# Other estimates of instruction time, by which a planned kernel orders its side work

## Chip, cores and metric

The kernel runs on one core of one Trainium2 chip. The metric is device time in microseconds (us) of one execution. The core has five engines with a queue each: TensorE (PE, matrix products into PSUM), VectorE (DVE), ScalarE (ACT), GpSimd (POOL) and SyncE (SP), which starts transfers.

## What is computed

One layer of a hybrid backbone for 1024 latent tokens and 256 context tokens of width 1024, in single precision. Cut to what matters:

```python
h_l = rmsnorm(x_l) * (1 + mod[1]) + mod[0]         # latents; h_c likewise for the context
parts = split(h @ w_in)                            # one combined input projection
lru = lru_branch(...)    # 8 blocks of 128 channels, both directions, first-order recurrence
gdn = gdn_branch(...)    # gated DeltaNet, 8 heads, chunks of 64, both directions
ssd = ssd_branch(...)    # Mamba-2 scan, 16 heads in 2 groups, chunks of 128, both directions
x_l = x_l + mod[2] * (sum(sigmoid(gate[k]) * (branch[k] @ w_branch[k]) for k in range(3)) @ w_out)
x_l = x_l + mod[5] * hier_moe(rmsnorm(x_l))        # top 2 of 32 experts, 1024 -> 512 -> 1024
out = rmsnorm(x_l)
```

In the gated DeltaNet each chunk solves a triangular system and then passes a 128x128 state on to the next chunk, so that the chunks of a head form a chain.

## The kernel before

A projection with single precision is made of three matmuls for each of 8 row tiles (high and low parts, names `hhi`, `hlo`, `whi`, `wlo`; PSUM tile `pj`, for the context `chi`, `clo` and `pjc`). A block is 128 columns of the weight: 48 matmuls of 512 columns for the latents, 24 of 256 for the context. These blocks are the main work of PE in the first part of the program (`phase1`): LRU blocks, context part of GDN, SSD group 0, SSD group 1, GDN heads, gates, merge. At most two latent PSUM tiles are held at a time.

All else there is side work, written as Python generators that yield between steps: convolutions (`conv`), LRU gates and scans (`lru_scan`: gate matmuls `psg`), inverses of the chunks' triangles (`gdn_inverse`: small matmuls `p`, `po`, `pz`), the chunk chains of a GDN head (`gdn_chain`, `gdn_steps`: matmuls `ch`, DVE steps `z`, `S`, `o`, ScalarE steps `w`), SSD tiles (`ssd_intra`: masks `gm` on GpSimd, matmuls `parg`, `py`, products `L`).

Which step stands where in the program is decided when the program is built, by `Clock`. Every engine call goes through a helper (L256, so that nearly all rows of the profile name this line), which first books an estimated time: an instruction starts when its engine, its inputs and its output buffer are free, and takes `cost`; its result is ready 0.1 us later. After every three projection matmuls of a row tile `mmblock` calls `tick`, which issues the next step of each side task whose last step, by the estimates, is done by PE's time:

```python
            g, r, m = e
            if r + m > clk.now:
                continue
```

Here `m` is `MARGIN` = -0.1 us and a new task begins with `r` = 0.0. Where PE's own work can't go on (both PSUM tiles held in `run`, a flag awaited in `until`, a stage's end in `drain`), `tick(True)` moves PE's estimated time on to the next side step. Everything issued to an engine's queue then runs in that order on the chip, whatever the real times are. The second part (routing, experts, combination) is ordered without these estimates.

Of the kernel before, what the change touches and what calls it, by code (L numbers as in the profile page):

```python
# [12 lines left out]
F32R = mybir.dt.float32r  # L13
# [5 lines left out]
PSUM = bass.MemoryType.PSUM  # L19
DRAM = bass.MemoryType.DRAM  # L20

P = 128
# [8 lines left out]
FX = 3  # L31
DB = 4
# [112 lines left out]
class Clock:  # L145
    """Estimated times (us) at which the engines and the tiles are free of the instructions issued so far; the order
    in which independent pieces of work are issued goes by them."""

    TABLES = (("Tanh", "Exp"), ("Gelu_apprx_tanh", "Tanh"), ("Silu", "Tanh"), ("Sqrt",), ("Sigmoid", "Tanh"))

# [13 lines left out]
    def cost(self, eng, op, out, kw, ins):  # L164
        n = out.free_size()
        if eng == "tensor":
            if op == "transpose":
                return 0.12
            c = kw["rhs"].free_size()
            return c / 2400 if kw["rhs"].dtype == F32R else max(4 * c / 2400, 0.06)  # L170
        if eng == "vector":
            if op == "reciprocal":
                return 0.07 + n * 6.3e-3
            if op == "tensor_reduce":
                n = ins[0].free_size()
            psum = any(a.space == PSUM for a in ins)
            fast = op in ("tensor_copy", "tensor_scalar") and not psum
            return (0.13 if psum else 0.07) + n * (0.53e-3 if fast else 1.05e-3)
        if eng == "scalar":
            f = str(kw.get("func")).split(".")[-1]  # L180
            c = 0.13 + 0.75e-3 * n
            if any(f in t for t in self.TABLES) and f not in self.table:
                self.table = next(t for t in self.TABLES if f in t)
                c += 1.28
            return c
        if op == "indirect_dma_start":
            return 1.0
        return 0.1 + n * {"tensor_tensor": 2.2e-3, "affine_select": 1.05e-3}.get(op, 3.5e-3)

    def issue(self, eng, op, args, kw):  # L190
# [13 lines left out]
        else:  # L204
            t += self.cost(eng, op, outs[0], kw, ins)
            self.t[eng] = t
            t += 0.1
# [10 lines left out]
class TimedPool:  # L218
    """a tile pool; keeps book of when the buffers that its tiles take over are free."""
# [50 lines left out]
class Core:  # L270
# [15 lines left out]
    # ---------------------------------------------------------------- consts  # L286
# [24 lines left out]
    def softplus(self, out, x, pool, shape, name):  # L311
        """max(x, 0) + log(1 + exp(-|x|)), the logarithm as 2 atanh(e / (2 + e))."""
# [20 lines left out]
    # ------------------------------------------------------------ projection  # L333
    def mmblock(self, ps, hi, lo, rhs, n, mid=None, kouter=False, gate=None):
        """ps[:, :n] = W^T @ rhs, W = hi + lo, rhs(k) = (hi, lo) of row tile k."""
# [16 lines left out]
    def run(self, jobs):  # L352
        """jobs: callables, or (weight block, kind, done); done(block, psum tile, is latent)."""
# [19 lines left out]
    def give(self, ps):  # L373
        """a projection's PSUM tile is not needed any more."""
        big = ps.free_size() == SEQ
        self.live[big] -= 1
        if not big:
            self.aux.free(ps)

    def bank(self, name):  # L380
        """a bank of PSUM that is kept across steps, until it is given back."""
# [4 lines left out]
    def room(self):  # L386
        """until a bank of PSUM is free."""
# [5 lines left out]
    def tick(self, idle=False):  # L393
        """next steps of the side tasks whose last steps are done by now; idle: the tensor engine has nothing else."""
# [26 lines left out]
    def take(self, pool, tag, n=1):  # L421
        """wait until n buffers of the tag are free, and count them as used until they are given back."""
# [13 lines left out]
    # ---------------------------------------------------------------- adaLN  # L436
    def mod_rows(self):
        """adaLN parts 2..5 of the latent stream, as rows in DRAM."""
# [44 lines left out]
    def start(self, xp):  # L483
        """adaLN scale and shift, norm, and the hi / lo parts of both transposed streams."""
# [121 lines left out]
    def gate_jobs(self, n):  # L606
        """jobs of the next n merge gate blocks."""
# [4 lines left out]
    # ------------------------------------------------------------------ LRU  # L612
# [14 lines left out]
    def lru_conv(self, b, ps, wts):  # L627
        """one block of 128 channels; columns: context, then latents."""
# [23 lines left out]
    def lru_scan(self, b, d, u, wts, hs):  # L652
        """gates and recurrence of one direction."""
# [80 lines left out]
    # ------------------------------------------------ decays, steps and betas  # L734
# [18 lines left out]
    def smalls(self, ps, n, t0, lat):  # L753
        """gate inputs of GDN and SSD for token tiles t0.. (tokens on partitions)."""
# [69 lines left out]
    def small_done(self):  # L824
        """the space of the gate inputs' temporaries goes to the merge gates."""
# [9 lines left out]
    # ------------------------------------------------------------------ SSD  # L835
# [9 lines left out]
    def ssd_block(self, b, ps, n, lat, dst, flag):  # L845
        """conv + silu of one xbc block, into a channel-major tile and / or token-major columns."""
# [34 lines left out]
    def ssd_update(self, pool, g, d, T, xs, bt, st):  # L881
        """state of direction d after token tile T (global tile index)."""
# [15 lines left out]
    def ssd_ctx_jobs(self, g):  # L898
        """context states of one group."""
# [35 lines left out]
    def ssd_intra(self, g, T, s, t0):  # L935
        """the part of a token tile's output that comes from the tile itself, both directions at once."""
# [46 lines left out]
        # 128 columns wide: the second half is overwritten by the head that it belongs to  # L983
# [6 lines left out]
    def ssd_scan(self, g, d, t0):  # L990
        """state chain of one direction and the output that comes from it."""
# [94 lines left out]
    def ssd_jobs(self, g, n):  # L1086
        """one group of 8 heads; n gate blocks run beside its scan."""
# [29 lines left out]
    # ------------------------------------------------------------------ GDN  # L1117
    def gdn_pool(self, tc, lat):
        """the context has room for two inverses at a time."""
# [9 lines left out]
    def gdn_fixed(self):  # L1129
        """lhsT tiles of the triangular inverses: zero outside the blocks that are written."""  # L1130
# [13 lines left out]
    def gdn_block(self, cb, ps, n, out, flag):  # L1144
        """conv + silu of one block into out [P, n]."""
# [8 lines left out]
    def gdn_keys(self, bt, norms=True, keys=True):  # L1154
        """token-major keys, their norms."""
# [36 lines left out]
    def gdn_decays(self, bt):  # L1192
        """decays between the tokens of a tile, both directions at once; the factors of keys by keys and queries."""
# [58 lines left out]
    def gdn_pre(self, bts, vflags, done):  # L1252
        """what two batches of 4 token tiles need that does not depend on the state; the inverses run beside."""
# [13 lines left out]
    def gdn_inverse(self, bt):  # L1267
        """Y = (I + B)^-1: 16-blocks by substitution, then block merges 16 -> 32 -> 64 -> 128."""
# [85 lines left out]
        # 32 -> 64; the forward direction fills the odd quadrants, the backward one the even ones  # L1354
# [29 lines left out]
        # 64 -> 128  # L1384
# [23 lines left out]
    def gdn_steps(self, sts):  # L1408
        """one token tile of every scan of sts, in step: the products first, then all that reads them."""
# [52 lines left out]
    def gdn_ctx_proj(self):  # L1462
        """context keys and values of all heads, kept in DRAM."""
# [11 lines left out]
    def gdn_ctx_jobs(self):  # L1475
        """context states of all heads."""
# [36 lines left out]
    def gdn_chain(self, h, bts, og):  # L1513
        """the scans of a head; og: outputs of the tiles 0, 1, 6 and 7, and of the tiles between, which are done first."""
# [31 lines left out]
    def gdn_out(self, h, bts, og, zs):  # L1546
        """norm and output gate of a head."""
# [35 lines left out]
    def gdn_jobs(self, n):  # L1583
        """n[0] gate blocks beside the preparation of the first head, n[1 + h] beside the scan of head h."""
# [57 lines left out]
    # ---------------------------------------------------------------- merge  # L1642
# [134 lines left out]
    # ------------------------------------------------------------------ MoE  # L1777
# [31 lines left out]
    def route_tokens(self, a, b):  # L1809
        """groups, experts and weights of the token tiles a to b - 1."""  # L1810
# [48 lines left out]
    def route(self, rp):  # L1859
        """slots of the assignments.  # L1860
# [656 lines left out]
```

## Time and profile before

| what | before |
| --- | --- |
| median of 3 runs | 3391.51 us (3386.56 to 3393.18) |
| profiled execution, span from its first to its last instruction | 3387.1 us |
| the same execution against the runs' median | 4.4 us below it |
| PE busy | 2976.2 us, 88% |
| DVE busy | 2251.0 us, 66% |
| ACT busy | 1553.5 us, 46% |
| POOL busy | 772.1 us, 23% |
| mean granted TensorE clock | 0.935 of full speed |

The page gives no time for the profiled execution other than its span, so the span stands for it. Busy shares are averages over stages which differ much; the rows further down are cut by stretch. A matmul's recorded duration includes the time in which the next already runs, so the rate of PE is read from the starts of two neighbours.

### The profile page before, as it was taken

The page shows a single profiled execution, that of the slowest core. Times are in us where ns is not written, and L with a number is a line of the kernel's source. Part 1 is how long each engine was busy: PE and PEld are TensorE (multiplying, and loading weights), DVE is VectorE, ACT ScalarE, POOL GpSimd, SP SyncE. Part 2 cuts the span into 40 slices and gives each one's busy share as a digit, 9 for nine tenths or more (in the row PEclk, how much of TensorE's full clock was granted, in tenths as well). Part 3 has the DMA queues.
Part 4 walks back from the last instruction along what each step waited for, and adds up shares of the span by engine and source line. Part 5 has one row for each costly group of instructions (what it writes and reads, how often), then busy time and mean ns, then how long its engine had stood idle before and what let it go on. Part 6 is the DMA issues. An engine that isn't in the chain of part 4 may idle for free. (4 is left out here: it accounts for less than half of the span.)

```text
span 3387.1 us, 48583 instructions
## 1 busy us (share of the span) xinstructions
PE 2976.2 (88%) x18570; PEld 2345.0 (69%) x18570; DVE 2251.0 (66%) x5049; ACT 1553.5 (46%) x2188; POOL 772.1 (23%) x662
## 2 busy tenths in 40 slices
PE   7878789879799789879989999899988799999992
PEld 3657667667568557668777778677766588878882
DVE  4676765753744745887988885244544887787786
ACT  4556565424315324454444444311121576676674
POOL 1121221202612611112111111212110243333333
PEclk8989999979799799989999999999989799999996
DMA  4112222201002001001010111454443697887896
GB/s 187 63 56 78 74 76 78 78 24 50 13 32 75 7 26 62 28 21 35 22 34 27 34 47 65 153 195 174 150 145 136 260 361 290 310 337 287 321 354 235
DMA packets 105531, 423.12 MB, mean 125 GB/s; under 512 B 17224, under 2 KB 26568, under 8 KB 79696
## 3 DMA queue, kind: packets, MB, share of 16 engines
q1 hardware_dynamic: 79872, 372.17, 30.5%
q10 hardware_dynamic: 13968, 26.83, 2.1%
q0 software_dynamic: 11456, 21.00, 1.7%
q8 instruction: 147, 2.41, 0.3%
q14 instruction: 88, 0.72, 0.1%
HBM read 381.11 MB, written 59.79 MB: 130 GB/s over the span
## 5 line engine op out<-in xcount | busy, mean ns | idle before, releaser
L256 PE MATMUL pj<-hhi,whi 128*128 128x512 f32 x1488 | 643.8, 433 | 17.8 <-DVE kq L256 10.3
L256 PE MATMUL pj<-hhi,wlo 128*128 128x512 f32 x1488 | 597.7, 402 | 6.9 <-POOL wlo L256 3.7
L256 PE MATMUL pj<-hlo,whi 128*128 128x512 f32 x1488 | 597.4, 401 | 0.0
L256 DVE TENSOR_TENSOR wl<-raw,wh 128x2048 fp32r<-128x2048 f32 x188 | 447.9, 2403 | 103.4 <-ACT wh L256 101.1
L256 POOL TENSOR_TENSOR wlo<-raw,whi 128x1024 fp32r<-128x1024 f32 x78 | 197.1, 2527 | 1002.8 <-ACT whi L256 985.5
L256 ACT ACTIVATE wh<-raw 128x2048 fp32r<-128x2048 f32 x188 | 360.6, 1919 | 129.2 <-PE psu L256 103.2
L256 PEld LDWEIGHTS pj<-hhi,whi 128*128 128x128 f32 x1488 | 286.7, 193 | 77.8 <-issue 10.1
L256 PEld LDWEIGHTS pj<-hhi,wlo 128*128 128x128 f32 x1488 | 285.3, 192 | 78.4 <-POOL wlo L256 5.3
L256 PEld LDWEIGHTS pj<-hlo,whi 128*128 128x128 f32 x1488 | 287.6, 193 | 53.8 <-issue 3.2
L256 ACT ACTIVATE whi<-raw 128x1024 fp32r<-128x1024 f32 x145 | 152.8, 1056 | 293.6 <-PE pj L256 212.8
L256 PE MATMUL psu<-wl,xh 128*128 128x512 f32 x576 | 226.6, 393 | 2.9 <-DVE wl L256 2.9
L256 PE MATMUL psu<-wh,xh 128*128 128x512 f32 x576 | 229.1, 398 | 0.0
L256 PE MATMUL psu<-wh,xl 128*128 128x512 f32 x576 | 226.0, 392 | 1.1 <-DVE xl L256 1.1
L256 ACT ACT_TABLE_LOAD x147 | 188.6, 1283 | 77.0 <-DVE xt L256 32.2
L256 DVE TENSOR_TENSOR wlo<-raw,whi 128x1024 fp32r<-128x1024 f32 x67 | 87.8, 1310 | 185.0 <-ACT whi L256 185.0
L256 ACT ACTIVATE w<-ch,D 128x128 f32<-128x128 f32 x288 | 84.7, 366 | 161.6 <-PE ch L256 155.7
L256 POOL TENSOR_TENSOR yo<-yo,m 128x1024 f32<-128x1024 f32 x35 | 103.6, 2961 | 183.5 <-ACT yo L256 183.4
L256 PE MATMUL psg<-u,lw 128*128 128x512 f32 (+1 forms) x192 | 89.8, 605 | 55.5 <-issue 52.7
L256 PE MATMUL pj<-bh,whi 128*128 128x512 f32 x384 | 122.9, 402 | 12.0 <-DVE acc L256 6.5
L256 PE MATMUL pj<-bl,whi 128*128 128x512 f32 x384 | 122.2, 400 | 8.9 <-POOL bl L256 6.3
L256 PEld LDWEIGHTS psu<-wl,xh 128*128 128x128 f32 x576 | 109.0, 189 | 29.3 <-DVE wl L256 8.0
L256 PEld LDWEIGHTS psu<-wh,xl 128*128 128x128 f32 x576 | 108.8, 189 | 24.7 <-DVE xl L256 1.8
(455 smaller groups left out, 6295.5 us busy)
## 6 DMA issues: line engine op xcount, KB each, us to landing
raw<-in_w SPq DMA_DIRECT2D x188, 1024.0 KB, 6.8
raw<-in_w_in SPq DMA_DIRECT2D x119, 512.0 KB, 3.5
wr<-in_w_mod SPq DMA_DIRECT2D x32, 512.0 KB, 6.0
gate<-gt ACTq DMA_DIRECT2D x48, 256.0 KB, 2.0
raw<-in_w_branch SPq DMA_DIRECT2D x24, 512.0 KB, 3.6
st<-br SPq DMA_DIRECT2D x24, 512.0 KB, 5.5
gt<-gate SPq DMA_DIRECT2D x24, 512.0 KB, 4.5
wm<-in_w_mod SPq DMA_DIRECT2D x8, 1024.0 KB, 5.7
```

What stands on the lines that cost most here:

```text
L256: return f(*args, **kw)
```

## The change

`Clock.cost` gets other formulas, and the time after which a result counts as ready becomes one of each engine. Nothing else in the program's logic changes; the lists of jobs, `MARGIN` and the pools stay. All instructions but one are the same in kind and number (the program has 148 table loads on ScalarE where it had 147); they stand in another order.

```diff
+    LAG = {"tensor": 0.21, "vector": 0.11, "scalar": 0.12, "gpsimd": 0.1, "sync": 0.1}
...
             if op == "transpose":
-                return 0.12
+                return 0.11
             c = kw["rhs"].free_size()
-            return c / 2400 if kw["rhs"].dtype == F32R else max(4 * c / 2400, 0.06)
+            if kw["rhs"].dtype == F32R:
+                return c / 2400 + 0.014
+            rows = kw["lhsT"].partition_size()
+            if "tile_position" in kw:
+                return 0.024 if rows == 32 else 0.055
+            return max(c / 600, 0.11)
+        psum = any(a.space == PSUM for a in ins)
...
+            if op == "tensor_tensor_scan":
+                return 0.08 + n * 2.08e-3
...
-            psum = any(a.space == PSUM for a in ins)
-            fast = op in ("tensor_copy", "tensor_scalar") and not psum
-            return (0.13 if psum else 0.07) + n * (0.53e-3 if fast else 1.05e-3)
...
+            if op in ("tensor_copy", "tensor_scalar", "memset"):
+                c = 0.14 if len(ins) > 1 else 0.09
+                return c + n * (1.04e-3 if psum else 0.52e-3)
+            c = 0.15 if op == "scalar_tensor_tensor" and len(ins) > 2 else 0.09
+            return c + n * 1.04e-3
...
-            c = 0.13 + 0.75e-3 * n
+            c = (0.08 if psum else 0.12) + 0.09 * max(0, len(ins) - 1) + 0.83e-3 * n
+            if kw.get("accum_out") is not None:
+                c += 0.2
...
-                c += 1.28
+                c += 1.38
...
-        return 0.1 + n * {"tensor_tensor": 2.2e-3, "affine_select": 1.05e-3}.get(op, 3.5e-3)
+        if op == "affine_select":
+            return 0.12 + n * 0.9e-3
+        return 0.15 + n * (2.25e-3 if op == "tensor_tensor" else 3.5e-3)
...
-            t += 0.1
+            t += self.LAG[eng]
```

What this moves is seen on PE at three places; the rows are in program order, `pj` and `pjc` are projection matmuls, and the others are side work.

The first place is the fifth LRU head's first gate matmul `psg`. Before, it stands in the middle of a block, after 999 projection matmuls, and the second gate follows one row tile later:

```order
L256 MATMUL pj<-hhi,wlo 128x512
L256 MATMUL psg<-u,lw 128x512 x2
L256 MATMUL psg<-u,lw 128x256
L256 MATMUL pj<-hhi,whi 128x512
L256 MATMUL pj<-hlo,whi 128x512
L256 MATMUL pj<-hhi,wlo 128x512
L256 MATMUL ptr<-ident,xt 128x128 x4
L256 MATMUL psg<-u,lw 128x512 x2
L256 MATMUL psg<-u,lw 128x256
```

In the changed order both stand behind 1032 projection matmuls, at the end of a latent block, and context matmuls follow:

```order
L276 MATMUL pj<-hhi,wlo 128x512
L276 MATMUL psg<-u,lw 128x512 x2
L276 MATMUL psg<-u,lw 128x256
L276 MATMUL ptr<-ident,xt 128x128 x2
L276 MATMUL psg<-u,lw 128x512 x2
L276 MATMUL psg<-u,lw 128x256
L276 MATMUL pjc<-chi,whi 128x256
L276 MATMUL pjc<-clo,whi 128x256
```

So 33 projection matmuls moved ahead of `psg`, and the two gates of the head stand together behind them.

The second place is the end of SSD group 0's projections. Before, the first two tiles' products `py` stand between the last row tiles:

```order
L256 MATMUL parg<-gm,mr 128x512 x4
L256 MATMUL pj<-hhi,whi 128x512
L256 MATMUL pj<-hlo,whi 128x512
L256 MATMUL pj<-hhi,wlo 128x512
L256 MATMUL py<-xs,L 128x128 x7
L256 MATMUL py<-xs,L 128x64
L256 MATMUL pj<-hhi,whi 128x512
L256 MATMUL pj<-hlo,whi 128x512
L256 MATMUL pj<-hhi,wlo 128x512
L256 MATMUL py<-xs,L 128x128 x7
L256 MATMUL py<-xs,L 128x64
```

In the changed order `py` stands behind the last projection matmul of the group, with the next tiles' `pcb` and `pcs` behind it:

```order
L276 MATMUL parg<-gm,mr 128x512 x4
L276 MATMUL pj<-hhi,whi 128x512
L276 MATMUL pj<-hlo,whi 128x512
L276 MATMUL pj<-hhi,wlo 128x512
L276 MATMUL parg<-gm,mr 128x512 x4
L276 MATMUL py<-xs,L 128x128 x7
L276 MATMUL py<-xs,L 128x64
L276 MATMUL py<-xs,L 128x128 x7
L276 MATMUL py<-xs,L 128x64
L276 MATMUL pcb<-cT,bT 128x128
L276 MATMUL pcs<-sst_178,cT 128x512
L276 MATMUL pcb<-cT,bT 128x128
```

So `py` of the first tiles moved behind the last 12 projection matmuls.

The third place is in the GDN stage, around a block's end after 4200 projection matmuls; `ch` belongs to the chain of one head, `p`, `pq` and `pk` to the next head's preparation. Before, single steps of the chain stand between row tiles ahead of it:

```order
L256 MATMUL ch<-z,Yf_8914 128x128
L256 MATMUL pj<-hhi,whi 128x512
L256 MATMUL pj<-hlo,whi 128x512
L256 MATMUL pj<-hhi,wlo 128x512
L256 MATMUL ch<-w_13635,kt 128x128
L256 MATMUL ch<-w,am 128x128
L256 MATMUL pq<-ident,kq 128x128 x4
L256 MATMUL p_13655<-Z_8917,B 64x64 x8
L256 MATMUL pj<-hhi,whi 128x512
L256 MATMUL pj<-hlo,whi 128x512
L256 MATMUL pj<-hhi,wlo 128x512
L256 MATMUL pk<-ident,kq 128x128 x4
```

In the changed order several steps of the chain stand behind one another at the block's end:

```order
L276 MATMUL pj<-hhi,wlo 128x512
L276 MATMUL ch<-w_13491,kt 128x128
L276 MATMUL ch<-w,am 128x128
L276 MATMUL pot<-ident,o 128x128 x4
L276 MATMUL ch<-S,kq 128x128 x2
L276 MATMUL pq<-ident,kq 128x128 x4
L276 MATMUL ch<-S,kq 128x128 x2
L276 MATMUL p_13591<-Z_13542,B 32x32 x16
L276 MATMUL ch<-z,Yf_8913 128x128
L276 MATMUL pk<-ident,kq 128x128 x4
L276 MATMUL ch<-w_13611,kt 128x128
L276 MATMUL ch<-w,am 128x128
```

So the chain's steps moved from places between projection matmuls to the block's end, where no projection matmul lies between them.

## Rows read from the trace of the kernel before

**Rows 1.** The page: busy time by engine, and the granted clock in 40 slices.
```profile
PE 2976.2 (88%) x18570; PEld 2345.0 (69%) x18570; DVE 2251.0 (66%) x5049; ACT 1553.5 (46%) x2188; POOL 772.1 (23%) x662
PEclk8989999979799799989999999999989799999996
```

**Rows 2.** Busy time by stretch: start:end length, busy us (instructions) by engine, PEclk, DMA.
```profile
40.00:537.00 497.00, 413.65 (x2011) 320.36 (x2011) 337.94 (x432) 285.95 (x374) 96.33 (x44) 0.91 0.21 67
690.00:756.00 66.00, 41.20 (x660) 35.11 (x660) 34.84 (x181) 16.57 (x52) 0.00 (x0) 0.69 0.07 21
867.00:955.00 88.00, 63.22 (x196) 37.41 (x196) 71.87 (x122) 19.64 (x53) 49.64 (x58) 0.78 0.04 12
1330.00:2040.00 710.00, 637.95 (x6902) 518.99 (x6901) 613.02 (x2668) 328.37 (x643) 119.68 (x208) 0.96 0.10 31
1430.00:1530.00 100.00, 79.64 (x1083) 64.92 (x1072) 89.78 (x421) 50.66 (x103) 14.84 (x31) 0.90 0.08 24
1530.00:1630.00 100.00, 99.29 (x840) 82.25 (x832) 78.42 (x297) 43.60 (x87) 21.11 (x34) 1.00 0.11 34
1272.00:2128.00 856.00, 782.30 (x7890) 639.95 (x7889) 681.52 (x2867) 390.73 (x754) 145.16 (x244) 0.97 0.11 36
```

**Rows 3.** Waits of PE, whole run: us in total, times, longest us.
```profile
PE psg L256 <- issue: 52.7, 7, 13.8
```

**Rows 4.** Timeline around psg: start, us, engine, operation [idle before <-releaser].
```profile
357.09 1.52 DVE L256 SCALAR_TENSOR_TENSOR u<-pjc,pp,u 128x254 f32<-128x254 f32 x3 [1.00 <-ACT u L256]
...
358.71 3.75 PE L256 MATMUL psg<-u,lw 128*128 128x512 f32 x4 [13.80 <-issue]
```

**Rows 5.** Waits of PE, then one of DVE, 1272 to 2128 us.
```profile
PE ch L256 <- DVE o L256: 25.1, 26, 3.7
PE pj L256 <- DVE kq L256: 10.3, 3, 6.8
PE pz L256 <- DVE B L256: 4.9, 1, 4.9
PE pz L256 <- DVE at L256: 4.4, 2, 2.5
...
PE ch L256 <- ACT w L256: 2.0, 4, 0.6
...
DVE z L256 <- PE ch L256: 22.8, 21, 10.2
```

**Rows 6.** Waits of PE, 610 to 691 us.
```profile
PE p L256 <- DVE Bc L256: 3.6, 1, 3.6
PE p L256 <- DVE Z L256: 3.4, 5, 1.0
PE p L256 <- DVE Zq L256: 3.1, 1, 3.1
```

**Rows 7.** Timeline of the SSD drain's rounds, POOL and PE.
```profile
853.55 1.27 POOL L256 TENSOR_TENSOR L<-L,t 128x512 f32<-128x512 f32 x1 [2.89 <-ACT L L256]
...
854.87 1.38 PE L256 MATMUL py<-xs,L 128*128 128x128 f32 x10 [0.55 <-POOL L L256]
...
877.54 6.14 PE L256 MATMUL py<-xs,L 128*128 128x128 f32 x32 [2.88 <-POOL L L256]
```

**Rows 8.** Groups by form, 40 to 2517 us; then PE's timeline.
```profile
L256 DVE TENSOR_TENSOR_SCAN ea<-ea,gate 128x1280 f32<-128x1280 f32 x8 | 22.5, 2810 | 0.0
...
L256 DVE SCALAR_TENSOR_TENSOR z<-ch,ge,vp 128x128 f32<-128x128 f32 x144 | 48.6, 344 | 27.3 <-PE ch L256 26.9
...
L256 ACT ACTIVATE w<-ch,D 128x128 f32<-128x128 f32 x288 | 84.7, 366 | 161.6 <-PE ch L256 155.7 <-DMA sgd<-Sc 5.5
...
L256 POOL TENSOR_SCALAR_AFFINE_SELECT gm<-shi 128x512 fp32r<-128x512 f32 x64 | 46.5, 726 | 5.0 <-PE parg L256 5.0
...
341.25 0.40 PE L256 MATMUL pj<-hhi,whi 128*128 128x512 f32 x1
...
341.72 0.39 PE L256 MATMUL pj<-hhi,wlo 128*128 128x512 f32 x1
```

More of the change, by code (lines that the diff above doesn't have):

```diff
@@ L173, in cost @@
                 return 0.07 + n * 6.3e-3
+            if op == "tensor_tensor_scan":
+                return 0.08 + n * 2.08e-3
             if op == "tensor_reduce":
-                n = ins[0].free_size()
-            psum = any(a.space == PSUM for a in ins)
-            fast = op in ("tensor_copy", "tensor_scalar") and not psum
-            return (0.13 if psum else 0.07) + n * (0.53e-3 if fast else 1.05e-3)
+                return 0.08 + ins[0].free_size() * 1.04e-3
+            if op == "stream_shuffle":
+                return 0.13 + n * 1.0e-3
+            if op in ("tensor_copy", "tensor_scalar", "memset"):
[3 more added lines that the diff above has]
+            return c + n * 1.04e-3
         if eng == "scalar":
             f = str(kw.get("func")).split(".")[-1]
-            c = 0.13 + 0.75e-3 * n
+            c = (0.08 if psum else 0.12) + 0.09 * max(0, len(ins) - 1) + 0.83e-3 * n
+            if kw.get("accum_out") is not None:
+                c += 0.2
             if any(f in t for t in self.TABLES) and f not in self.table:
                 self.table = next(t for t in self.TABLES if f in t)
-                c += 1.28
+                c += 1.38
             return c
```

## Prediction

> **What bounds the kernel now.** I read the page first, then busy time by stretch, the waits of TensorE (PE), the waits of VectorE (DVE), and last the timeline around the longest waits. On the page PE is busy 2976.2 of 3387.1 us and DVE 2251.0 [rows 1], so PE looks like the bound; but that is an average. By stretch the picture differs [rows 2]. From 40 to 537 us (projections with the LRU beside them) PE is busy 413.65 of 497 us and DVE 337.94. In the drain from 690 to 756 us no projection is left and a chain of small matmuls and DVE steps runs alone: PE 41.20 of 66 us, granted clock 0.69. The same holds for the SSD drain, 867 to 955 us, clock 0.78 (1118 to 1205 us is its copy for the second group). In the GDN stage, 1330 to 2040 us, both engines are close to full: PE 637.95 and DVE 613.02 of 710 us. What the changed numbers can win is the waiting of PE at side instructions that stand too early in its queue, since the projection matmuls behind them wait too; what they can lose is that a side chain starts or ends later where it alone sets the end of a stage. The routing, the experts and the combination (2600 us to the end) don't issue by the estimates, and I take them as unchanged.
>
> **The change, part by part.** The new lines are slower almost throughout, and they slow the side engines more than PE. A projection matmul of 512 columns starts 0.235 us after the one before [rows 8]; the old formula gives 512/2400 = 0.213, the new one 0.227. A DVE scan of 1280 takes 2.810 us; old 0.07 + 1280 x 0.00105 = 1.41, new 0.08 + 1280 x 0.00208 = 2.74. The DVE step z takes 0.344; old 0.26, new 0.28. The ScalarE step w takes 0.366; old 0.23, new 0.28. One line goes the other way: a GpSimd mask of 512 takes 0.726 on average; old 0.64, new 0.58. A result of PE now counts as ready 0.21 us after its end instead of 0.1. So in the estimates DVE work lengthens by more than projections do, and a side step is put behind more projection matmuls than before. No instruction is added but one table load on ScalarE (147 to 148 in the built programs); ScalarE is busy 1553.5 of 3387.1 us [rows 1], so I charge nothing for it, and if nothing covered it, it would cost one load, about a microsecond, below what counts here.
>
> **LRU.** Seven times the first gate matmul psg of a head waits, 52.7 us in all, longest 13.8 [rows 3]. The timeline shows why: at 358.71 us psg starts after an idle time of 13.80 us, just behind the end of the context convolution on DVE, which starts its last part at 357.09 [rows 4]. The new table would put psg behind that wait if it were allowed to. But a new side task enters the list with an estimated end of 0.0, and its first gate comes out right after the convolution's last step was issued; the estimates only decide what DVE work was put ahead of the convolution. I priced the DVE work that stands ahead of it in the new order with durations of the trace: about 3.5, 3.3, 5, 9.8, 8, 1, 9.5 and 12.5 us of waiting for the eight heads, 52.6 in all. I take **-1 us**; bounds -12 (the fourth and fifth lose a good half of their wait) and +8 (the order of the two scans of a head turns against it once).
>
> **Context part of GDN.** Between 610 and 691 us PE waits 3.6, 3.4 and 3.1 us at p matmuls [rows 6], 10.1 in all. In the new order the first group of these stands 48 projection matmuls later (48 x 0.235 = 11.3 us), so these waits go. But the stretch behind is the uncovered drain, and now 348 instead of 328 small matmuls stand in it. The drain's 66 us for 328 matmuls make 0.2 us for each, so 20 more cost 4 us; a batch that starts 11.3 us later may end the stage up to 4 us later still, of which I take all. I take -10.1 + 8 = **-2 us**; bounds -10.1 (the drain's own chain decides) and +6 (the late batch decides: the 16 us of both together, less the 10).
>
> **SSD.** The first two matmul groups py of the drain's chain start at 854.87 us, while projections still run; the next round starts at 877.54 [rows 7], so a round takes some 23 us and the drain is a chain of them: GpSimd's product L ends (853.55 + 1.27), py starts. The first parg stands 12 to 15 projection matmuls later in the new order and py behind the last projection, not 12 ahead of it. PE loses nothing by that, but the chain starts 12 x 0.235 = 2.8 us later, and the rounds behind it are as long as before. I take +2.5 for each of two groups, **+5 us**; bounds 0 (the wait of 0.55 us ahead of py and the projections moved forward hide it) and +8.
>
> **GDN heads.** PE's waits that the order makes are those on o (25.1 us), kq (10.3), B (4.9), at (4.4) and w (2.0) [rows 5], 46.7 us. DVE in turn waits 22.8 us for ch. If every one of these steps stood where its input is ready, 46.7 us would be won; that is the lower bound. Against it, the chain of a head (80 steps ch) spans 1226 projection matmuls in the new order over heads 1 to 7 where it spanned 1064, 162 more or 162 x 0.235 = 38 us, and side matmuls behind the last projection matmul of a block, where nothing covers them, rise from 467 to 891. If this length is paid in full, and only half of the waits other than kq (which is late by itself) come back, the sum is 38 - 18 = +20: the upper bound. The two ends are far apart. DVE is busy 86% of the stage, which leaves neither end whole: 97 us of idle are there to be won from, but the stage can't run much ahead of DVE. I take the middle, -13.
>
> **Merge.** The side work there is DMA-fed modulation rows, priced as before: 0.
>
> **Sum.** -1 - 2 + 5 - 13 = -11 us. Against the profiled execution that is 3387.1 - 11 = 3376.1 of span; the median of the runs, 3391.51, lies 4.4 above that span, so **3380 us**.
>
> **The rivals.** (a) The waits only move. Where a block's last projection is done and its PSUM isn't free, PE waits anyway; 891 side matmuls at block ends could be just the old waits, seen at another place. DVE at 613.02 of 710 us speaks for it, the 46.7 us of PE waits with projections behind them against it. Then GDN gives about 0, and the sum is +2: 3393, no change that can be told.
> (b) Slower: longer chains set the stage ends. The point where it decides is the GDN chain: if a head's chain is paid at its new length, 38 us, and the waits in front of ch come back to half, +20, then with the others the sum is -1 + 6 + 5 + 20 = +30: 3421; with the GDN term at half of that, 3411. For it speaks that steps at the ends of blocks run uncovered, as the drains do; against it that the next head's projections usually wait for the same DVE.
> (c) The clock. Stretches in which PE pauses run slower: from 1430 to 1530 us PE is busy 79.64 us at clock 0.90, from 1530 to 1630 us 99.29 us at 1.00 [rows 2]. If the whole GDN stage fell to 0.90 from its mean of 0.96, PE would lose 0.06 x 710 = 43 us of matmul time, of which its 72 us of idle time absorb a part; I price half, +20, and with no gain left in GDN that is 3393 + 20 = 3413. The Trainium skill, "TensorE: Matmul & The Clock Gate", section "What's actually happening", says that an idle array is gated down from 2.4 to 1.2 GHz; the rows of the two stretches agree, since a granted share of 0.90 is a mix of the two levels. By that rule the 424 more side matmuls at block ends are a danger, and the forecast would come out on the slower side.
> (d) The gain is whole: with GDN near its lower bound, -40, the sum is -38 and the time 3353.
>
> **Chances.** My forecast, 3361 to 3385, 0.36; (d) and beyond, 0.10; (a), 3385 to 3398, 0.25; (b) 0.20; (c) 0.09. A change of under 0.2% (6.8 us) is about what a measurement of this kernel can't tell from none, so the bound between faster and same lies at 3384.7 and that to slower at 3398.3. Faster 0.46, same 0.25, slower 0.29. The likeliest case's own range is 3361 to 3385; the range that holds 8 in 10 leaves out most of (d)'s and the upper part of (b)'s ends: 3350 to 3412.
>
> **What would show it.** In the changed kernel's profile: waits of PE on o in the GDN stage at half of 25.1 us or less, with the stage shorter than 856 us from 1272 to 2128; psg's waits still some 50 us; the waits at p between 610 and 691 us gone and the drain behind them 4 to 8 us longer; first py of the SSD drain behind the last projection, with rounds of 23 us as before. I would be wrong if the ends of blocks in the GDN stage show PE idle for as long as the waits did (a), if the GDN stage is longer than 860 us with its waits gone (b), or if its granted clock falls under 0.94 (c).

## The result, and the profile after

The changed kernel takes 3429.72 us (3427.16 to 3431.9) where the one before takes 3391.74: 1.0117 times as long, 95% interval 1.0105 to 1.0129. That is 38 us slower, on the other side of the forecast and beyond its range. The profiled execution has a span of 3426.6 us.

The page of the changed kernel has nearly the same sums as [rows 1], PE busy 2988.3 us instead of 2976.2 and DVE 2255.8 instead of 2251.0:

```profile
PE 2988.3 (87%) x18570; PEld 2370.3 (69%) x18570; DVE 2255.8 (66%) x5049; ACT 1556.9 (45%) x2189; POOL 769.6 (22%) x662
...
PEclk9989999959799799989899989999989799999996
```

PE has the same 18570 matmuls and is busy 12 us longer with them, as much as its growth in the GDN heads alone (further down); the other 27 us of the 39 by which the span grew are idle time of PE. Where the loss lies is read by the starts of the same projection matmul in both traces (5304 of them, in the same order in both). The table is worked out from the two timelines; "drain" is the time from a stage's last projection matmul to the first of the next stage.

| up to projection matmul | before, us | changed, us | difference | stage's own share |
| --- | --- | --- | --- | --- |
| 1008 (fifth LRU block) | 368.1 | 344.6 | -23.4 | |
| 1656 (LRU done) | 536.7 | 536.7 | 0.0 | 0.0 |
| 2136 (context part of GDN done) | 756.2 | 757.9 | +1.6 | +1.6 (drain 65.5, then 83.4) |
| 3096 (SSD done) | 1204.9 | 1210.2 | +5.4 | +3.8 (first drain 88.6, then 101.1) |
| 3480 (GDN heads begin) | 1321.3 | 1326.5 | +5.2 | -0.2 |
| 5112 (GDN heads nearly done) | 2109.1 | 2139.3 | +30.2 | +25.0 |
| 5303 (last) | 2161.8 | 2192.1 | +30.3 | +0.1 |
| end | 3387.1 | 3426.6 | +39.4 | +9.1 |

Two rows need care. At 1008 the changed kernel hasn't yet had the fifth head's psg wait: before, it stands at 999 (13.8 us), now at 1032 (7.3 us). From 1044 on the changed kernel is 10.9 us ahead, at 1620 it is 4.4, and then the last head's psg waits 13.8 us instead of 6.1. Of the last row's 9.1 us most is scatter, as a run of the old order shows further down.

The same stretches in busy time, as in [rows 2]: LRU, the longer drain of the context part, the first SSD drain, and the heads from 3480 to 5112:

```profile
40.00:537.00 497.00, 410.39 (x2005) 320.41 (x2006) 338.84 (x433) 284.70 (x373) 96.49 (x44) 0.91 0.21 68
674.43:757.86 83.43, 52.32 (x690) 45.16 (x689) 47.88 (x264) 18.58 (x58) 1.27 (x2) 0.59 0.05 17
856.79:957.88 101.09, 73.15 (x254) 43.62 (x253) 83.41 (x141) 25.26 (x69) 58.63 (x69) 0.80 0.04 11
1326.50:2139.30 812.80, 726.09 (x7546) 605.68 (x7544) 656.75 (x2801) 362.69 (x710) 132.33 (x229) 0.93 0.10 32
```

and for comparison the heads before, cut at the same two matmuls:

```profile
1321.30:2109.10 787.80, 714.10 (x7550) 583.28 (x7548) 651.94 (x2803) 361.35 (x712) 132.61 (x229) 0.96 0.10 34
```

The reader is to see that DVE has almost the same work in the heads, 656.75 and 651.94 us, and that its idle time grew from 135.9 to 156.1 us. PE is busy 726.09 us instead of 714.10 and its granted clock fell from 0.96 to 0.93. The heads hold two thirds of the loss.

PE's waits in the heads (PE, what it waits for: us in total, times, longest) answer to [rows 5]:

```profile
PE ch L276 <- DVE o L276: 16.8, 13, 2.7
PE pj L276 <- DVE kq L276: 16.7, 4, 7.9
PE ch L276 <- ACT w L276: 9.8, 13, 1.9
...
PE pz L276 <- DVE at L276: 6.3, 3, 3.7
```

The wait for o fell from 25.1 to 16.8 us, by a third where the prediction looked for half; kq rose from 10.3 to 16.7, w from 2.0 to 9.8 and at from 4.4 to 6.3. The wait for B at pz is gone. So the five waits that the prediction added up, 46.7 us before, are 49.6 now. On the other side DVE waits longer for the chain's matmuls. In the changed kernel, 3480 to 5112:

```profile
DVE z L276 <- PE ch L276: 28.7, 27, 8.2
DVE S L276 <- PE ch L276: 27.0, 27, 2.9
```

and before, the same stretch:

```profile
DVE z L256 <- PE ch L256: 21.2, 18, 10.2
...
DVE S L256 <- PE ch L256: 12.8, 16, 1.7
```

55.7 us now, 34.0 before: 21.7 us more, as much as DVE's idle time grew in all, with the other waits rising and falling among themselves. That these waits are the cause doesn't follow; the experiments with the chain come back to them.

Where PE's time went is seen best at one block's end. After projection matmul 3816 the changed kernel's PE timeline (start, duration, operation) reads

```profile
1467.64 0.40 PE L276 MATMUL pj<-hhi,wlo 128*128 128x512 f32 x1
1467.87 0.38 PE L276 MATMUL ch<-w,kt 128*128 128x128 f32 x2
...
1531.53 0.65 PE L276 MATMUL p<-Z,B 32*32 32x32 f32 x32
1533.30 1.11 PE L276 MATMUL pv<-ident,vT 128*128 128x128 f32 x4 [1.12 <-ACT P L276]
1534.21 1.06 PE L276 MATMUL ch<-S,kq 128*128 128x128 f32 x4
1534.92 0.77 PE L276 MATMUL pj<-hhi,whi 128*128 128x512 f32 x1
```

and before

```profile
1489.68 0.39 PE L256 MATMUL pj<-hhi,wlo 128*128 128x512 f32 x1
...
1516.90 0.71 PE L256 MATMUL pj<-hhi,whi 128*128 128x512 f32 x1
```

The next block's first projection matmul starts 67.3 us after this block's last one, and before 27.2 us. Behind the last one stands side work alone: chain steps and, as the last of it, the next head's p and pv. In that stretch PE is busy 46.22 of 68.90 us at clock 0.76, and DVE 61.85:

```profile
1466.00:1534.90 68.90, 46.22 (x694) 39.13 (x694) 61.85 (x311) 28.47 (x67) 8.77 (x20) 0.76 0.03 9
```

Summed over the 34 block ends between 3480 and 5112, the time above 0.235 us from one projection matmul to the next is 81 us before and 196 in the changed kernel; at all other places it is 325 and 235. **The change took 90 us out of the covered stretches and put 115 into the uncovered ones**, where covered means between the projection matmuls of a block. This time isn't all waiting, since it holds the side matmuls themselves. Worked out from the timelines:

| in the heads, us | before | changed |
| --- | --- | --- |
| between a block's projection matmuls | 698.5 | 608.6 |
| of it PE idle | 39.7 | 11.4 |
| of it DVE idle | 119.6 | 133.0 |
| granted clock | 0.97 | 0.97 |
| at the 34 block ends | 89.2 | 204.2 |
| of it PE idle | 34.0 | 75.3 |
| of it DVE busy | 72.9 | 181.1 |
| granted clock | 0.90 | 0.82 |

So of the 90 us 28 are idle time of PE and 62 are side matmuls that left; of the 115, 41 are idle time and 74 are side matmuls. With them 108 us of DVE's work moved to the block ends, where no projection runs beside it, and between the projections DVE is idle longer than before although that part is 90 us shorter.

The waits that the prediction named elsewhere: psg still waits 44.1 us (52.7 before, [rows 3]), and with all its waits of over 1 us, whatever they are put down to, 50.2 (53.9 before); the p waits of [rows 6] are gone, 0.3 us between 610 and 674 us:

```profile
PE psg L276 <- issue: 44.1, 6, 13.8
```

```profile
PE p L276 <- ACT P L276: 0.3, 1, 0.3
```

and the SSD drain begins with py at 858.54 us with a first round of 22.3 us, where [rows 7] had 854.87 and 22.7:

```profile
858.54 2.00 PE L276 MATMUL py<-xs,L 128*128 128x128 f32 x16 [0.43 <-POOL L L276]
...
880.83 1.43 PE L276 MATMUL py<-xs,L 128*128 128x128 f32 x5 [4.29 <-POOL L L276]
```

### The profile page after: what moved, and what is told of

The parts are those of the page before. It is cut to its first block, busy times and chain, and to the rows that moved or that the text cites. A ratio compares the mean times of both kernels' runs of the same rounds, so it can differ in the third digit from the quotient of the medians.

```text
span 3426.6 us, 48578 instructions
## 1 busy us (share of the span) xinstructions
PE 2988.3 (87%) x18570; PEld 2370.3 (69%) x18570; DVE 2255.8 (66%) x5049; ACT 1556.9 (45%) x2189; POOL 769.6 (22%) x662
## 3 DMA queue, kind: packets, MB, share of 16 engines
q1 hardware_dynamic: 79872, 372.17, 30.2%
## 5 line engine op out<-in xcount | busy, mean ns | idle before, releaser
L276 PE MATMUL pj<-hhi,whi 128*128 128x512 f32 x1488 | 640.7, 431 | 25.3 <-DVE kq L276 16.7
L276 PE MATMUL psg<-u,lw 128*128 128x512 f32 (+1 forms) x192 | 87.5, 588 | 51.6 <-issue 44.1
L276 PE MATMUL pj<-bl,whi 128*128 128x512 f32 x384 | 122.6, 401 | 10.3 <-POOL bl L276 6.8
```

The costliest lines, as they stand in the source:

```text
L276: return f(*args, **kw)
```

## Experiments

Spans are given from projection matmul 3480 to 5112 as "heads"; the row under each run is that stretch (busy us by engine, granted clock).

**Which stage.** Two kernels use both tables, one the new table in the heads and the old elsewhere (its main lines follow), the other the reverse:

```diff
+        f = self.cost_new if self.fitted else self.cost_old
+        return f(eng, op, out, kw, ins)
...
-            t += self.LAG[eng]
+            t += self.LAG[eng] if self.fitted else 0.1
...
+                c.clk.fitted = True
                 if "gdn" in stages:
                     c.gdn_fixed()
```

New table in the heads alone. 

> The new formulas and lags are used only while the GDN heads are issued, the old ones elsewhere, so the GDN heads stand exactly as in the changed kernel and all else as in the one before. Theory (the loss is in the order of the GDN heads' side steps): the stage between the projection matmuls 3480 and 5112 takes 25 us longer than before and the whole 3415 +- 5 us. Rival (the heads only suffer from what the earlier stages leave behind, GpSimd and transfers): 3391 +- 5, and the stage is as long as before.

Measured 3418.35 us, ratio 1.0088 [1.0071, 1.0105]:

```profile
1319.30:2131.00 811.70, 724.50 (x7546) 603.65 (x7544) 656.53 (x2801) 362.57 (x710) 132.46 (x229) 0.93 0.10 33
```

New table everywhere but in the heads. 

> The other half: the new formulas everywhere in the first part but in the GDN heads, which stand as before. Theory: the 25 us of the heads are gone, and 5 us of the stages ahead and 9 us of the merge are left, 3405 +- 5 us. If the merge's 9 us are only a consequence of the longer GDN stage, 3397. Rival (the heads suffer from the earlier stages): near the changed kernel, 3425.

Measured 3406.22 us, ratio 1.0055 [1.0038, 1.0072]:

```profile
1326.20:2114.10 787.90, 714.08 (x7548) 583.27 (x7547) 651.88 (x2802) 361.28 (x712) 132.57 (x229) 0.97 0.11 34
```

The heads take 811.7 us in the one and 787.9 in the other, 24 us apart whatever came ahead of them: the loss is the heads' own order. Both theories held. The rest of the change costs 17 us by the second run; the runs on scatter and the merge, below, show how much of that is the merge's. By whole times the two lose 29.4 and 17.2 us, 46.6 together where the changed kernel loses 38.0; with intervals of some 6 us either way that is no proof that the parts add up, nor against it. The small shares of the table are no scatter: five kernels with the changed order there take 221.1 to 222.2 us for the context part and 452.2 to 453.9 for SSD, four with the old one 216.9 to 219.7 and 447.2 to 448.7.

**Which numbers.** One kernel keeps DVE's old formulas, one the old lag of 0.1 us; all else is new. The second one's line:

```diff
-    LAG = {"tensor": 0.21, "vector": 0.11, "scalar": 0.12, "gpsimd": 0.1, "sync": 0.1}
+    LAG = {"tensor": 0.1, "vector": 0.1, "scalar": 0.1, "gpsimd": 0.1, "sync": 0.1}
```

> All new formulas and lags but VectorE's, which are the old ones. In the order the side matmuls that stand behind the last projection matmul of a block in the GDN stage fall from 891 to 474 (467 before), 292 of them at the one end after 3816. Theory (longer estimates for VectorE put the steps that feed it behind more projection matmuls, VectorE runs dry in the covered parts and the rest is done uncovered at block ends): the GDN stage comes back to within 8 us of before, the whole 3400 +- 8 us. Rival (PE's lag of 0.21 us does it): no change against the changed kernel, 3428 +- 5.

Measured 3419.64 us, ratio 1.0094 [1.0077, 1.0110]; heads 801.0:

```profile
1324.00:2125.00 801.00, 717.96 (x7560) 595.78 (x7558) 659.84 (x2807) 360.23 (x710) 132.76 (x231) 0.94 0.10 33
```

> All new formulas with the old lag of 0.1 us for every engine. 773 side matmuls at block ends of the GDN stage. Theory (VectorE's formulas): still slow, 3422 +- 8 us. Rival (the lags, above all 0.21 us for PE, lengthen the estimated chain): 3400 +- 8.

Measured 3445.31 us, ratio 1.0166 [1.0149, 1.0183]; heads 814.9, and the LRU stage 15 us longer than in the changed kernel:

```profile
1339.10:2154.00 814.90, 730.39 (x7549) 603.42 (x7548) 655.14 (x2798) 355.28 (x706) 130.30 (x227) 0.93 0.10 32
```

In time both expectations missed, and both rivals too. By these profiles DVE's formulas account for about half of the heads' loss (13 of 25 us are left without them), not for nearly all; the profiled execution with DVE's old formulas was 7.7 us faster than its run's median, so the half is rough. The lags account for none of it; without the new ones the kernel is slower still.

**Is it the direction?** MARGIN shifts all side steps against PE's estimated time; more negative is earlier.

```diff
-MARGIN = -0.1
+MARGIN = -1.2
```

In the changed kernel, -1.2. 

> The changed kernel with MARGIN -1.2 in place of -0.1: every side step may stand 1.1 us of estimated time earlier. In the order the side matmuls behind the last projection matmul of a block of the GDN stage fall from 891 to 234 (467 before), and their mean place is that of before. Theory of direction (the new table puts steps too late): the GDN heads lose 8 us or less against before, the whole is 3400 +- 10 us. Rival (the lists of jobs and gate blocks fit the old order, and any other order loses): the heads still lose 15 to 30 us, the whole 3410 to 3430.

Measured 3432.32 us, ratio 1.0121 [1.0104, 1.0137]; the heads came back to 788.1 us, as the theory said; LRU, context part and SSD lost 29 us by matmul 3480 against the kernel before, so that the whole time met neither theory nor rival:

```profile
1350.30:2138.40 788.10, 719.79 (x7565) 582.05 (x7564) 653.47 (x2785) 368.66 (x720) 131.99 (x229) 0.97 0.10 33
```

In the kernel before, -0.4. 

> The kernel before with MARGIN -0.4: the steps of the old table 0.3 us earlier. 425 side matmuls at block ends of the GDN stage. Theory of direction: within 10 us of before in the GDN heads, perhaps faster, the whole 3380 to 3398 us. Rival (any other order loses): the heads lose 13 us or more, the whole 3404 or more.

Measured 3405.37 us, ratio 1.0043 [1.0026, 1.0059]; the heads 807.4, the stages ahead 9 us shorter than before; the numbers are the rival's:

```profile
1312.30:2119.70 807.40, 723.27 (x7576) 590.95 (x7575) 660.98 (x2809) 360.77 (x713) 132.03 (x229) 0.96 0.10 33
```

In the kernel before, -0.7. 

> The kernel before with MARGIN -0.7: 246 side matmuls at block ends of the GDN stage, their mean place 22 projection matmuls ahead of before. Theory of direction: block ends shrink, but more steps now stand ahead of their inputs, so between 10 us faster and 15 us slower than before in the heads. Rival (any other order loses): the heads lose 13 us or more.

Measured 3454.12 us, ratio 1.0184 [1.0167, 1.0201]; the heads 799.3, 11.5 us longer, inside the theory's wide range and short of the rival's 13; the stages ahead 25 us longer:

```profile
1346.00:2145.30 799.30, 723.07 (x7575) 589.28 (x7574) 661.73 (x2794) 340.92 (x697) 131.92 (x229) 0.96 0.10 33
```

In the kernel before, +0.3. 

> The kernel before with MARGIN +0.3: the steps of the old table 0.4 us later, the direction in which the change moves them. 496 side matmuls at block ends of the GDN stage, 212 of them behind 3816 (128 before, 332 changed). Theory of direction: the heads lose 5 to 20 us, the whole 3396 to 3411. Rival (any other order loses) gives the same here; it differs from the theory in the three runs beside this one.

Measured 3421.24 us, ratio 1.0097 [1.0080, 1.0114]; the heads 804.3, as expected, the whole time 10 us above:

```profile
1319.60:2123.90 804.30, 711.40 (x7516) 588.65 (x7514) 659.22 (x2793) 354.52 (x701) 131.33 (x226) 0.94 0.10 33
```

The new table's heads are healed by standing 1.1 us earlier, so there they stood too late. But the old table's heads lose in both directions, 16.5 us with steps later and 11.5 to 20 us with steps earlier: the old order lies in a hollow, and direction alone doesn't say what a shift does, as the run with -0.4 shows. The times of block ends and of all other places show the two sides of it (us above the projection pace, with PE's idle time in brackets, worked out from the timelines):

| kernel | heads | at block ends | elsewhere |
| --- | --- | --- | --- |
| before | 787.8 | 81 (34.0) | 325 (39.7) |
| changed | 812.8 | 196 (75.3) | 235 (11.4) |
| changed, -1.2 | 788.2 | 55 (22.3) | 352 (46.0) |
| before, -0.4 | 807.5 | 73 (28.8) | 353 (55.3) |
| before, -0.7 | 799.3 | 41 (15.3) | 377 (61.0) |
| before, +0.3 | 804.3 | 132 (59.2) | 291 (33.7) |

Later steps lengthen PE's idle time at block ends, earlier steps that between projections; no column alone orders the times of the heads.

**Which side work.** The chain of a head has its own margin, `CM`; the rest of the heads' side work takes the stage's.

```diff
-CM = None
+CM = -1.2
```

Only the chain earlier. 

> The changed kernel with a margin of -1.2 for the chain of a GDN head alone; all other side tasks (the next head's preparation, its inverses, the outputs) keep -0.1, and all other stages stand as in the changed kernel. In the order 684 side matmuls stand at block ends of the GDN stage (891 changed, 234 with -1.2 for all). Theory (VectorE waits for the chain's matmuls ch, 56 us in the changed kernel, 43 before and 37 with -1.2 for all; the chain's lateness is the loss): VectorE's waits for ch fall under 45 us, and the GDN stage is 8 us or less over before, the whole 3410 +- 6 us. Rival (the preparation's lateness is what fills the block ends): the waits for ch fall and the stage stays within 6 us of the changed kernel's 813 us, the whole 3428 +- 6.

Measured 3443.3 us, ratio 1.0148 [1.0132, 1.0165]; the heads 829.4, 17 us longer than in the changed kernel:

```profile
1326.80:2156.20 829.40, 736.32 (x7585) 595.66 (x7584) 656.16 (x2819) 370.53 (x723) 135.90 (x233) 0.95 0.10 32
```

The theory that the chain's lateness is the loss falls: moved alone it does harm. Its rival, 3428 us and a stage within 6 us of the changed kernel's, missed as well. DVE's waits for ch in the heads hardly moved, 53.5 us in this run and 55.7 in the changed kernel (the 43 before that the expectation names is for 1330 to 2140 us, past matmul 5112; at the same matmuls it is the 34.0 above):

```profile
DVE z L276 <- PE ch L276: 31.6, 29, 17.0
DVE S L276 <- PE ch L276: 21.9, 25, 2.1
```

In the run new_prep12, below, where the heads are short again, they are 57.2 us, so these waits don't decide the length:

```profile
DVE S L276 <- PE ch L276: 28.6, 30, 2.3
DVE z L276 <- PE ch L276: 28.6, 25, 12.3
```

Two more kernels put a margin on the heads alone, `c.margin`, and read it in `add`:

```diff
-        self.post.insert(0 if first else len(self.post), [gen, 0.0, MARGIN if margin is None else margin])
+        self.post.insert(0 if first else len(self.post), [gen, 0.0, self.margin if margin is None else margin])
...
+                c.margin = -1.2
                 if "gdn" in stages:
                     c.gdn_fixed()
```

All of the heads' side work. 

> The changed kernel with MARGIN -1.2 for all side tasks of the GDN heads (chain, preparation, outputs); the other stages stand as in the changed kernel. 234 side matmuls at block ends of the GDN stage, as with -1.2 everywhere, where that stage took 788.2 us against 787.8 before. Theory (in the heads the new table puts all steps too late together): the stage comes to 790 +- 5 us, the whole to 3405 +- 6 us. Rival (it did so only on the ground that the stages ahead with -1.2 had laid): 805 us or more, 3420 or more.

Measured 3409.59 us, ratio 1.0053 [1.0036, 1.0070]:

```profile
1334.20:2123.20 789.00, 721.01 (x7566) 582.93 (x7566) 654.01 (x2785) 368.51 (x720) 132.18 (x229) 0.97 0.10 33
```

All but the chain (`CM` = -0.1), so preparation, inverses and outputs. 

> The same with -1.2 for all but the chain, which keeps -0.1: preparation, inverses and outputs are issued early and the chain where the new table puts it. 593 side matmuls at block ends. Theory now (the preparation of the next head is what stands too late; the chain alone moved made it worse): the stage 795 +- 8 us, the whole 3410 +- 8. Rival (neither part alone does it; steps of both must keep pace with each other): the stage 805 us or more, the whole 3420 or more.

Measured 3417.41 us, ratio 1.0081 [1.0064, 1.0097]:

```profile
1332.60:2124.80 792.20, 711.77 (x7516) 591.43 (x7515) 641.63 (x2764) 359.03 (x705) 130.33 (x225) 0.93 0.11 33
```

The heads' recovery is their own (789.0 us in the first of these), and both theories held. All but the chain brings 792.2, but the edges of the stretch flatter it: some of its DVE work now lies behind matmul 5112 (641.63 us of DVE in the stretch), and in both runs 20 matmuls of the first preparation moved ahead of 3480. The fairer span is that from 3096 to 5303: 956.9 us before, 981.8 changed, 956.5 with all earlier, 966.8 with all but the chain earlier, and 994.1 with the chain earlier. So the side work other than the chain, moved alone, takes back 15 of the 25 us (by whole times 0.36 of 1.17%). The chain, which costs 12 us when it moves alone, takes back another 10 once the rest has moved: the parts don't add up, and the chain is part of the cure. Preparation and outputs weren't moved apart from each other.

**How much is scatter, and the merge.** The kernel before with MARGIN read from an attribute that is -0.1 everywhere:

> The kernel before in other words: MARGIN is read from an attribute that is -0.1 in every stage, so that every instruction stands as before. It shows how far two runs of the same order differ, whole and by stage. Every theory: ratio 1.000 within its interval; the stages within 2 us of before. If the merge differs by 7 us or more here, the 7 to 11 us that the merge lost in the other runs are no effect of an order.

Measured 3390.68 us, ratio 1.0002 [0.9993, 1.0011]. The starts up to the last projection matmul agree within 2.4 us and the heads' length within 0.3, but the merge (from the first start of `pj<-bh,whi` to the `pj<-bl,whi` behind its last) takes 315.8 us in this profile and 308.9 in that of before, with the same order:

```profile
2159.60:2475.40 315.80, 288.48 (x1166) 220.39 (x1165) 140.14 (x107) 56.65 (x56) 55.59 (x23) 0.96 0.48 171
```

So the bare 10 us that the changed kernel's merge seemed to lose, 318.9 against 308.9, are 3.1 against this profile, and the 9.1 us of the table's last row are 2.0. The new table from the last gate blocks on alone:

> The new formulas and lags only from the last gate blocks and the merge on; all stages ahead stand as before. Theory (the modulation rows' VectorE steps, which the new table puts up to 90 matmuls earlier, stand in front of those that free the merge's PSUM): the merge is 10 us longer, the whole 3398 to 3402 us. Rival (the merge only suffers from what the stages ahead leave): the merge as before, 3390 +- 3.

Measured 3396.24 us, ratio 1.0018 [1.0009, 1.0027], 6 us slower; the merge takes 317.4 us. The time lies between the two expectations: the order from the last gate blocks on costs something, 3 to 9 us by the interval of the times; the profiles of this pair differ by 1.6 us in the merge, so where those us lie isn't shown.

**A faster version.** The heads hardly feel what came ahead of them, so the earlier LRU and SSD of the run with -0.4 can be had without its heads (the old table, main lines alone):

```diff
+    margin = -0.4
...
+                    c.margin = -0.1
                     if J["gc"]:
...
+                    c.margin = -0.4
                     c.run(J["ssd"])
...
+                c.margin = -0.1
                 if "gdn" in stages:
```

> The kernel before with MARGIN -0.4 in the LRU and SSD stages alone, -0.1 in the context part of GDN, the GDN heads and the merge, which stand as before. In the run with -0.4 everywhere the LRU stage was 6 us and the SSD stages 7 us shorter than before, and the heads lost 20. Theory (stages add up, each with a best earliness of its own): 3 to 13 us faster, 3378 to 3388. Rival (those 13 us are scatter between orders and runs): no change, 3391 +- 4.

Measured 3376.71 us, ratio 0.9959 [0.9946, 0.9973]: faster than both kernels, and a little beyond the theory's 3378. Against the profile of before it is 5 us ahead after LRU, 11.4 after SSD and 12.8 at the end of the projections. LRU in this kernel, to be held against [rows 2]:

```profile
40.00:531.70 491.70, 412.33 (x2012) 323.01 (x2011) 334.22 (x432) 281.94 (x371) 92.69 (x43) 0.92 0.21 67
```

## Why the prediction was wrong, step by step

**The likeliest case failed in one term, the GDN heads.** The step reads "If every one of these steps stood where its input is ready, 46.7 us would be won; that is the lower bound", and sets against it 38 us for the longer chain; "I take the middle, -13". Measured is +25.0, beyond the upper bound of +20. Two things were wrong in it. The waits weren't a sum to be won: the five that it added up came to 49.6 us. Over all its waits PE did lose 28 us of idle time between projections, but it gained 41 at block ends, because the side work that left the covered part, with 108 us of DVE's steps, had to be done there with no projection beside it. That exchange, 90 us out and 115 in, has no term in the sum. And the price of the delay was sought in the chain, by its length in projection matmuls. The runs show that the rest of the side work, the next head's preparation with its outputs, matters more: moved early alone it takes back 15 of 25 us, while the chain moved early alone costs 12 more by matmul 5303; both together take back all 25. The prediction counted the right thing, 467 against 891 side matmuls at block ends, and then priced it as equal to the waits in rival (a).

**LRU, -1 forecast, 0.0 measured.** Right, and by its mechanism: psg's waits come to 50.2 us where 52.6 were worked out, and head by head they are 3.0, 3.8, 4.7, 8.5, 7.3, under 1, 9.1 and 13.8. What the term didn't say is that the stage would be 10.9 us ahead on the way and give it back by the last head.

**Context part, -2 forecast, +1.6 measured.** The waits at p left as said, 10.1 us to 0.3, and the last projection matmul comes earlier, at 674.4 instead of 690.7 us. The drain grew from 65.5 to 83.4 us. So both parts were larger than worked out, -16.3 instead of -10.1 and +17.9 instead of +8, and that the bounds held is due to their cancelling.

**SSD, +5 forecast, +3.8 measured.** Right in the sum: py comes 2.0 us later counted from the start of the stage, and the rounds are as long as before. The two groups lose 0.8 and 2.9 us. Here too the projections end earlier (856.8 for 866.8 us in the first group) and the drains, 101.1 and 101.5 us for 88.6 and 87.0, take it back.

**Merge, 0 forecast, about +6 by the times of tail_new.** The modulation rows do move, 6 to 90 matmuls earlier; I had them as unchanged. That these rows are what costs the time isn't shown.

The measured terms, 0.0 + 1.6 + 3.8 + 25.0 + 6, make 36 of the 38 us.

**The rivals.** (b) named the right sign and a time of 3421, with a chance of 0.20; its mechanism, a head's chain paid at its new length, isn't what the runs support. The stated range, up to 3412, left out this rival's own time. (a)'s mechanism, waits that move to block ends, is what happened, but the exchange isn't even. (c)'s sign came true, the clock fell from 0.96 to 0.93, under the 0.94 named, but it can't carry the loss: with MARGIN -0.4 the heads take 807.4 us at 0.96 and with all but the chain earlier 792.2 us at 0.93, so the clock doesn't order the times. Between the projections the clock is the same, 0.97 in both kernels. At the block ends, where it fell from 0.90 to 0.82, DVE is busy 181.1 of 204.2 us; with the same work standing there a faster PE could take away at most the other 23, and before they were 16. That (c)'s part is zero isn't shown; no run kept PE's clock up in such a stretch.

**What stays open.** Why the side work other than the chain matters most is only argued, from the code: a V tile (`vc`) exists once, and the next head's V block can't give its PSUM back before `pv` has read the last one; pv and one chain step stand right ahead of the resumed projection in the timeline above. No run gives this tile a second buffer. Nor is it shown why the kernel before loses 20 us in the heads with steps only 0.3 us earlier; PE's idle time between projections is 15.6 us longer there, and which steps wait too early wasn't followed up.

## What to carry to other kernels

Estimates that lie nearer to the trace don't by themselves make a better order. Here the greedy rule on top of them keeps PE from waiting, while in the heads DVE's work sets how long the block ends last. A wait taken away under cover is a gain only if the work that was delayed for it isn't due before the next point at which the covering engine must stop; count what stands at those points, and price it as uncovered. Test a scheduling table by stage: the heads took the same time whatever stood ahead of them, so one kernel with the table in one stage located the loss, and a margin chosen by stage, with the old table, found a faster kernel than either. Within a stage the parts didn't add up, so move them together before giving one the blame.

## What the runs showed of the hardware

The old order of instructions came back within 0.4 us in the GDN heads (787.8, 787.5 and 787.9 us in three kernels) and the changed one within 1.1 (812.8 and 811.7), while the LRU stage took 534.6 to 538.3 us in four kernels with the same order, and the merge, whose blocks read gates and branches from DRAM, differed by 6.9 us between two profiles of the same order. A difference of some us there needs more than one profile. Why the merge scatters more isn't shown.
